# RWKV stage: the chunk's inverse folded into the state-side operand before the recurrence, so that a step leaves the product stream twice

## The chip, the cores and the metric

One core of one Trainium2 chip runs the whole program. The metric is the device time of one execution in microseconds (us), median of several runs.

## The reference, cut to what matters

One inference step of a hybrid backbone on 512 sample tokens and 128 prompt tokens (640 in all, 2048 wide): a large input product, two branches (RWKV-7 with 16 heads of 64, and an RG-LRU), gates, output products and norms. The change is in the RWKV branch, which runs forward and backward over the tokens of each head:

```python
def step(s, inp):
    r_t, w_t, k_t, v_t, kk_t, a_t = inp
    s_kk = jnp.einsum('bhvk,bhk->bhv', s, kk_t)
    s = s * w_t[:, :, None, :] - s_kk[..., None] * (kk_t * a_t)[:, :, None, :] + v_t[..., None] * k_t[:, :, None, :]
    return s, jnp.einsum('bhvk,bhk->bhv', s, r_t)
```

The kernel computes this by chunks of 64 tokens. In a chunk the vectors u (what each token takes from the state and from the tokens before it) solve a triangular system: u = Q (N S + M V), with S the state at the chunk's start, V the values, M a masked matrix of tokens against tokens, and Q the inverse of a unit triangular 64x64 matrix. With u known, the new state and the outputs y are plain products.

## The kernel before, in words

The program is one stream of large products on PE with all other work hung into it by hand. `piece` issues six matmuls for each 128 rows of a product's depth (L327: three of the split pairs high x high, high x low, low x high, each for two halves of 320 tokens), and then calls `tick`, which gives one turn to each of three queues of Python generators: `front` (mixing r, k, v), `side` (the recurrence `rwkv`) and `back` (`normed`, which prepares the next pair of heads, and `norm`, which finishes the last one). A generator that says `yield from idle(n)` lets n turns pass. So the numbers in W, INV, QI, X1 to X3 (before) or W, MV, MX, IW, INV, QI, X1, X2 (after) are turns between two pieces of side work, and they set the order of every engine's instructions. Each engine works its own list strictly in that order; SP issues nearly all transfers, in its own order too. A product of depth 2048 has 16 turns.

The RWKV stage goes through eight pairs of heads, i = 0 to 7. Pair i is worked while the products of host i run: for i = 1 to 5 these are seven (three gates m, r, k and v of the next pair, and ga), 112 turns; host 0 has nine, host 6 eight, host 7 seven (six gates and ga). `rwkv(i)` is put on `side` when host i begins.

What `rwkv(i)` does before the change, in this order:
- The decayed operands are written to `st4` (L835, L836), in pieces.
- `values`: ten transposes of v (L983) and copies into `sv`.
- `first` (L930) multiplies b against both decayed operands, 128 columns, six times; `bring` masks the two halves (L936, L937) into `at` and `rb`. `send` writes `at` to DRAM.
- The blocks are read back to `xn` and `xi`, 32x32 blocks on 104 partitions, which ScalarE turns (L1064, L1067). VectorE inverts them by 30 rounds of two instructions (L1072, L1074). Between the rounds `second` (L948, masked by L954) and `turned` (L964) are worked, for the k side.
- The inverses go out (L1081, L1085) and come back (L1093, L1099); two rounds of 32x32 products (L1108, L1122) make the whole Q in `qm`.
- Eight steps of the recurrence, forward and backward chunks at once (four chunks and heads wide in the first two steps, two wide after). A step leaves the product stream three times: `px` and part of `py` (L1141, L1145), then a copy `xt_` (L1148) and `pu` = Q x (L1153), then `pn` (L1162) and the rest of `py` (L1166). Copies by `put` (L1000, L1001) hand u and the state on.

On PE "an excursion" below is one such departure from the stream of L327 and the return to it. PSUM has four one-bank buffers `rw` for all of this. A line shown as x16 for fp32 operands is eight matmuls in the program: each is recorded as two.

Of the kernel before, what the change touches and what calls it, by code (L numbers as in the profile page):

```python
# [45 lines left out]
W = (2, 2, 2, 2, 2, 2, 2, 2, 2, 1, 3, 2)  # L46
INV = (0, 1, 1, 1, 1, 1, 1, 1, 2, 2, 2, 2, 2, 2, 2, 2)
QI = (1, 5, 7, 3, 1)
X1 = (1, 2, 1, 1, 2, 1, 1, 1)
X2 = (2, 2, 2, 2, 2, 1, 2, 2)  # L50
X3 = (3, 2, 2, 2, 3, 1, 2, 1)
NI = (1, 2, 1, 1)

# [10 lines left out]
C_ID, C_MSK, C_SEL, C_SCAN = 0, 128, 384, 386  # L64
# [6 lines left out]
def _consts():  # L71
    c = np.zeros((P, C_END), np.float32)
    p = np.arange(P)
    j = (p % CH)[:, None]
    t = np.arange(CH)[None, :]
    c[:, C_ID:C_ID + P] = np.eye(P)
    c[:, C_BLK:C_BLK + P] = (p[:, None] // CH == p[None, :] // CH)
    c[:, C_MSK:C_MSK + 256] = np.concatenate([j < t, j <= t, j > t, j >= t], 1)
    c[:, C_SEL:C_SEL + 2] = p[:, None] % 32 == np.arange(2)[None, :]
    c[:, C_SCAN:C_SCAN + CH] = t != 0  # L80
    return c
# [53 lines left out]
def step_kernel(ctx: ExitStack, tc: tile.TileContext, xt, w_in, w_a, w_b, w_o, ws, lw2, ada_w, ada_g, ada_b, cond, condr, gains,  # L135
# [569 lines left out]
    with tc.tile_pool(name="rwkv", bufs=1) as rp:  # L705
        def slot(name, dtype=F32):
            return rp.tile([P, SLOT], dtype, tag="rs", name=name, bufs=13)

        def mixed(q, i):
# [17 lines left out]
            def mix():  # L727
# [7 lines left out]
                s = slot("sh")  # L735
                sv = chunks(s)
                V.tensor_tensor(sv[:, 0:8], zr[:, :, 0:64], zr[:, :, 2:66], ALU.add)
                yield
                V.tensor_tensor(sv[:, 1:8], sv[:, 1:8], zr[:, 0:7, 1:65], ALU.add)
                yield  # L740
                V.tensor_tensor(sv[:, 0:7], sv[:, 0:7], zr[:, 1:8, 1:65], ALU.add)
                yield
                V.tensor_tensor(s[:, TS:T], zp[:, 0:128], zp[:, 2:130], ALU.add)
                V.scalar_tensor_tensor(o[:, :TS], s[:, :TS], dc(3 + q, i), o[:, :TS], ALU.mult, ALU.add)
                V.scalar_tensor_tensor(o[:, TS:T], s[:, TS:T], dc(6 + q, i), o[:, TS:T], ALU.mult, ALU.add)
# [11 lines left out]
        mask = [c[:, C_MSK + P * d:C_MSK + P * (d + 1)].rearrange("p (a t) -> p a t", a=2) for d in range(2)]  # L757
# [12 lines left out]
        class Scan:  # L770


            def __init__(self, i, k, r):
                self.i, self.k, self.r, self.nk = i, k, r, None
                self.th, self.pin, self.pex, self.kd, self.bk, self.st4 = ([None, None] for _ in range(6))
# [54 lines left out]
            def decayed(self, d, n0=0, n1=NC):  # L830

                n = slice(n0, n1)
                for e in range(2):
                    sl = hd(e)
                    V.tensor_tensor(self.st4[d][sl, n, e, 0], chunks(self.nk)[sl, n], self.pex[d][sl, n], ALU.mult)  # L835
                    V.tensor_tensor(self.st4[d][sl, n, e, 1], chunks(self.r)[sl, n], self.pin[d][sl, n], ALU.mult)  # L836
# [20 lines left out]
        def normed(i, k, r):  # L857
# [49 lines left out]
            z.bonus = kds  # L907
            ready[i] = z

        def rwkv(i, v):  # L910
# [6 lines left out]
            st4s = z.st4 = [rp.tile([P, NC, 2, 2, CH], F32, tag=f"st4{d}", name="st4") for d in range(2)]  # L917
            rbs = [rp.tile([P, NC, CH], F32, tag=f"rb{d}", name="rb") for d in range(2)]
            toks = [rp.tile([P, NC, 2, CH], F32, tag=f"tok{d}", name="tok") for d in range(2)]
            ats = [None, None]  # L920
            pcs = z.pcs

            def first(d, n0):

                nn = min(4, NC - n0)
                pa, m = ps1(), nn * P
                for n in range(n0, n0 + nn):
                    x = P * (n - n0)
                    for e in range(2):
                        PE.matmul(pa[hd(e), x:x + P], z.bk[d][hd(e), n, e],  # L930
                                  st4s[d][hd(e), n, e].rearrange("p a t -> p (a t)"), start=True, stop=True)

                def bring():
                    mb = mask[d].unsqueeze(1).to_broadcast([P, nn, 2, CH])
                    pav = pa[:, :m].rearrange("p (c a t) -> p c a t", a=2, t=CH)
                    V.tensor_tensor(chunks(ats[d])[:, n0:n0 + nn], pav[:, :, 0], mb[:, :, 0], ALU.mult)  # L936
                    V.tensor_tensor(rbs[d][:, n0:n0 + nn], pav[:, :, 1], mb[:, :, 1], ALU.mult)  # L937
# [3 lines left out]
            def second(d, n0):  # L941

                nn = min(4, NC - n0)
                pb, m = ps1(), nn * P
                for n in range(n0, n0 + nn):
                    x = P * (n - n0)
                    for e in range(2):
                        PE.matmul(pb[hd(1 - e), x:x + P], z.bk[d][hd(e), n, 1 - e],  # L948
                                  st4s[d][hd(e), n, e].rearrange("p a t -> p (a t)"), start=True, stop=True)

                def bring(e):
                    mb = mask[d].unsqueeze(1).to_broadcast([P, nn, 2, CH])
                    so = hd(1 - e)
                    V.tensor_tensor(st4s[d][so, n0:n0 + nn, e],  # L954
                                    pb[so, :m].rearrange("p (c a t) -> p c a t", a=2, t=CH), mb[so], ALU.mult)

                return lambda: bring(0), lambda: bring(1)
# [120 lines left out]
            for _ in work:  # L1078
                pass
# [363 lines left out]
```

## Time and profile before

| what | value |
|---|---|
| median of three runs | 2220.9 us (2217.12 to 2221.93) |
| the profiled execution: its time, its span | 2224.06 us, 2222.3 us |
| mean granted TensorE clock | 0.979 of 2.4 GHz |
| busy: PE, DVE, ACT, POOL | 2102.0, 1373.5, 976.0, 876.1 us |

The span runs from the first to the last instruction; 1.8 us lie around it. Busy time of PE counts modelled ends of pipelined matmuls, so a stretch in which PE is "busy" throughout can still hold lost time, and starts of successive instructions are the better measure.

### The profile page before, as it was taken

What the parts mean: (1) busy time and instruction counts of PE and PEld (TensorE: products, weight loads), DVE (VectorE), ACT (ScalarE), POOL (GpSimd) and SP (SyncE); (2) the same over time, 40 slices, a digit from 0 to 9 for tenths busy, and PEclk for the clock granted to TensorE, in tenths of its full rate; (3) what the DMA queues carried; (4) which work ended last, traced back from release to release, by engine and by line L of the source; (5) the groups of instructions that cost most, each with busy time, mean ns of one, the idle gap of its engine ahead of it and who ended that gap; (6) DMA issues with size and microseconds to landing.
All of it is one profiled execution on the core that took longest, in us unless ns stands there. A gap on an engine that the chain in (4) does not pass through costs nothing.

```text
span 2222.3 us, 47521 instructions
## 1 busy us (share of the span) xinstructions
PE 2102.0 (95%) x18236; PEld 1960.5 (88%) x18236; DVE 1373.5 (62%) x2665; ACT 976.0 (44%) x2264; POOL 876.1 (39%) x1164
## 2 busy tenths in 40 slices
PE   3999999999998998998998989989999899999997
PEld 2789999998888898898888888989988799999997
DVE  5655765696747756666676477665532699733354
ACT  4336776643433444444334434444333422234554
POOL 1244545553333333433333333334323455543343
PEclk8999999999999999999999999999999899999999
DMA  8953334332322222223123232232222766644474
GB/s 335 337 183 133 119 115 137 97 99 75 97 67 77 92 81 84 72 77 95 60 74 99 76 92 71 78 88 79 87 85 75 251 223 227 186 147 154 151 240 154
DMA packets 203507, 281.64 MB, mean 127 GB/s; under 512 B 69360, under 2 KB 91056, under 8 KB 202768
## 3 DMA queue, kind: packets, MB, share of 16 engines
q1 hardware_dynamic: 202832, 277.38, 39.2%
q8 instruction: 144, 2.36, 0.4%
q0 software_dynamic: 448, 1.23, 0.2%
q14 instruction: 83, 0.68, 0.1%
HBM read 237.70 MB, written 39.85 MB: 125 GB/s over the span
## 4 chain that ended last, share of the span: by engine, by line
PE 71%; DVE 19%; DMA 4%; issue 3%; ACT 2%; SPq 1%; POOL 1%; DVEq 0%; ACTq 0%; POOLq 0%
PE pj L327 52%; DVE tmp L1072 3%; DVE xi L1074 3%; PE rw L563 3%; DVE junk L1321 2%; PE rw L479 2%; PE rw L930 2%; DVE gws L1323 1%; DVE st L954 1%; PE ada L381 1%; PE pj L479 1%; PE rw L1153 1%; PE rw L1141 1%; PE rw L1166 1%; PE rw L948 1%
## 5 line engine op out<-in xcount | busy, mean ns | idle before, releaser
L310 POOL TENSOR_TENSOR wl<-wr,wh 128x256 fp32r<-128x256 f32 x922 | 790.9, 866 | 1255.8 <-ACT wh L309 1199.9
L327 PE MATMUL pj<-xh,wh 128*128 128x320 f32 (+2 forms) x2976 | 761.8, 323 | 2.3 <-ACT wh L309 2.3
L327 PE MATMUL pj<-xh,wl 128*128 128x320 f32 (+2 forms) x2976 | 724.5, 311 | 2.0 <-DVE wl L310 1.5
L327 PE MATMUL pj<-xl,wh 128*128 128x320 f32 (+2 forms) x2976 | 724.8, 311 | 0.0
L309 ACT ACTIVATE wh<-wr 128x256 fp32r<-128x256 f32 x1048 | 421.4, 413 | 517.4 <-PE pj L327 396.5
L327 PEld LDWEIGHTS pj<-xh,wh 128*128 128x128 f32 x2976 | 502.9, 190 | 34.5 <-issue 14.3
L327 PEld LDWEIGHTS pj<-xh,wl 128*128 128x128 f32 x2976 | 512.8, 189 | 3.7 <-DVE wl L310 2.5
L327 PEld LDWEIGHTS pj<-xl,wh 128*128 128x128 f32 x2976 | 513.3, 189 | 0.1
L1072 DVE TENSOR_TENSOR tmp<-xn,xi 104x30 f32<-104x30 f32 (+14 forms) x240 | 100.0, 417 | 82.6 <-ACT xn L1067 76.1
L1001 DVE COPY sv<-rw 64x128 f32<-64x128 f32 x80 | 23.6, 295 | 198.0 <-ACT sv L1000 196.8
L310 DVE TENSOR_TENSOR wl<-wr,wh 128x256 fp32r<-128x256 f32 x126 | 57.6, 459 | 127.1 <-ACT wh L309 126.9
L1074 DVE TENSOR_TENSOR xi<-xi,tmp 104x30 f32<-104x30 f32 (+14 forms) x240 | 99.9, 416 | 8.2
L1321 DVE SCALAR_TENSOR_TENSOR junk<-gws,cb 128x512 f32<-128x512 f32 x64 | 67.5, 1055 | 10.1 <-ACT cb L1313 10.1
L327 PE MATMUL pj<-yah,wh 128*128 128x320 f32 x256 | 59.6, 315 | 8.1 <-ACT g L1234 8.1
L954 DVE TENSOR_TENSOR st<-rw,c 64x512 f32<-64x512 f32 (+1 forms) x96 | 57.6, 600 | 12.4 <-PE rw L948 10.2
L1323 DVE SCALAR_TENSOR_TENSOR gws<-gws,cb 128x512 f32<-128x512 f32 x64 | 61.5, 961 | 1.9
L327 PE MATMUL pj<-yah,wl 128*128 128x320 f32 x256 | 59.4, 314 | 0.5 <-POOL wl L310 0.5
L327 PE MATMUL pj<-yal,wh 128*128 128x320 f32 x256 | 59.2, 313 | 0.0
L327 PE MATMUL pj<-ybh,wh 128*128 128x320 f32 x256 | 58.5, 310 | 0.4 <-DVE thx L1357 0.4
L327 PE MATMUL pj<-ybh,wl 128*128 128x320 f32 x256 | 58.5, 309 | 0.3 <-POOL wl L310 0.3
L327 PE MATMUL pj<-ybl,wh 128*128 128x320 f32 x256 | 58.3, 309 | 0.0
L1000 ACT ACTIVATE sv<-rw 64x128 f32<-64x128 f32 x80 | 21.7, 271 | 74.7 <-PE rw L1153 68.9
(767 smaller groups left out, 3077.6 us busy)
## 6 DMA issues: line engine op xcount, KB each, us to landing
wr<-w_in SPq DMA_DIRECT2D x312, 256.0 KB
adaw<-ada_w SPq DMA_DIRECT2D x64, 512.0 KB
wr<-w_o SPq DMA_DIRECT2D x128, 256.0 KB
gws<-ada_g SPq DMA_DIRECT2D x64, 256.0 KB
thl<-th SPq DMA_DIRECT2D x32, 320.0 KB
th<-thl SPq DMA_DIRECT2D x32, 320.0 KB
thm<-g SPq DMA_DIRECT2D x64, 160.0 KB
thx<-thm SPq DMA_DIRECT2D x32, 320.0 KB
```

The costliest lines, as they stand in the source:

```text
L309: S.activation(h, r, AF.Copy)
L310: lows[pos[1] % len(lows)].tensor_tensor(lo, r, h.bitcast(F32), ALU.subtract)
L327: PE.matmul(p[:, :t1 - t0], w, x[:, t0:t1], start=(k == 0 and a == 0), stop=(k == nk - 1 and a == 2))
L479: PE.matmul(p[:, :HT], u[:, w], x[:, t], start=new, stop=end)
L563: PE.matmul(p, a, b, start=(n == 0), stop=(n == 2))
L930: PE.matmul(pa[hd(e), x:x + P], z.bk[d][hd(e), n, e], st4s[d][hd(e), n, e].rearrange("p a t -> p (a t)"), start=True, stop=True)
L954: V.tensor_tensor(st4s[d][so, n0:n0 + nn, e], pb[so, :m].rearrange("p (c a t) -> p c a t", a=2, t=CH), mb[so], ALU.mult)
L1001: V.tensor_copy(sv[hd(1), a, 1], src[hd(1), b])
L1072: V.tensor_tensor(t, xn[:NV, j, j + 1:].unsqueeze(2).to_broadcast([NV, m, j]), xi[:NV, j, :j].unsqueeze(1).to_broadcast([NV, m, j]), ALU.mult)
L1074: V.tensor_tensor(xi[:NV, j + 1:, :j], xi[:NV, j + 1:, :j], t, ALU.add)
L1321: V.scalar_tensor_tensor(junk, w, 1.0, cbs[h][:, 0], ALU.mult, ALU.mult, accum_out=gs[:, h, n, 0:1])
L1323: V.scalar_tensor_tensor(w, w, 1.0, cbs[h][:, 1], ALU.mult, ALU.mult, accum_out=gs[:, h, n, 1:2])
```

## The change

The inverse Q is multiplied into the operand [N^T; M^T] of each chunk ahead of the recurrence (`fold`), for all chunks. A step then gets u in one product of depth 128 from state and values together (`pu`), and the copy `xt_` is gone; all the rest of the step is one more excursion. The state's part of y is a product of its own now with a decayed r (`z.rp`). `first` makes 64 columns; the other products of tokens against tokens are made by `across` and `outward`, for which b and k of both heads stand in one stationary operand where that can be; a second mask `smk` lets the unmasked state side through. `decayed` is done once for whole rows in `normed`. The mixing of r, k, v is written with multiply-adds into the result and without the buffer `sh`. All turn counts are new; `turned` is moved behind the inverse.

Turns of `rwkv(i)` counted from these tuples, from its start: before, the inverse begins at turn 24, its write (L1085) is at 48, the reads at 53, L1108 at 60, the first step at 64, the end at 105. After: `first` at 0 and 2, `across` at 5, 7, 9 and 12, the inverse at 11, `outward` at 17, 22, 28 and 45, the write at 45, the reads at 47, L1108 at 51, `fold` and `turned` from 55, the first step at 63, the end at 100.

```diff
+W, SD, LD = (2, 0), 0, (1, 3)
+MV, MX = (1, 2, 2, 2), 2
+IW = (2, 5, 7, 9)
+INV = (0, 1, 1, 2, 2, 3, 2, 3, 3, 2, 3, 3, 2, 2, 2, 2)
+QI = (1, 2, 4, 2, 2, 1, 1, 1)
+X1 = (2, 2, 2, 2, 1, 2, 1, 2)
+X2 = (3, 3, 3, 3, 3, 3, 3, 2)
...
+                ov, m4, m2 = chunks(o), dc(3 + q, i), dc(6 + q, i)
+                for x, y in ((ov[:, 0:8], zr[:, :, 0:64]), (ov[:, 0:8], zr[:, :, 2:66]), (ov[:, 1:8], zr[:, 0:7, 1:65]),
+                             (ov[:, 0:7], zr[:, 1:8, 1:65])):
+                    V.scalar_tensor_tensor(x, y, m4, x, ALU.mult, ALU.add)
+                    yield
...
+            def decayed(self, d):
+
+                t = self.r if d else slot("rp")
+                V.tensor_tensor(chunks(t), chunks(self.r), self.pin[d], ALU.mult)
+                V.tensor_tensor(self.pex[d], chunks(self.nk), self.pex[d], ALU.mult)
+                self.rp[d], self.nkp[d] = chunks(t), self.pex[d]
...
+            def both(n0):
+                for n in range(n0, n0 + 5):
+                    for e in range(2):
+                        yield n, e, slice(CH * (n - n0), CH * (n - n0 + 1))
...
             def first(d, n0):
+                pa = ps1()
+                for n, e, x in both(n0):
+                    PE.matmul(pa[hd(e), x], z.bk[d][hd(e), n, e], z.nkp[d][hd(e), n], start=True, stop=True)
                 def bring():
+                    V.tensor_tensor(ats[d][:, n0:n0 + 5], five(pa), wide(mask[d][:, 0]), ALU.mult)
...
+            def across(d, n0):
+                pq = [ps1(), ps1()]
+                for n, e, x in both(n0):
+                    PE.matmul(pq[e][hd(e), x], z.nkp[d][hd(e), n], ident[hd(e), hd(e)], start=True, stop=True)
+                for n, e, x in both(n0):
+                    PE.matmul(pq[1 - e][hd(e), x], z.nkp[d][hd(e), n], z.bk[d][hd(e), n, 1 - e], start=True, stop=True)
+                for h in range(2):
+                    V.tensor_tensor(sws[d][:, n0:n0 + 5, h], five(pq[h]), wide(smk[d][:, h]), ALU.mult)
+
+            def outward(d, n0):
+                po = [ps1(), ps1()]
+                for n, e, x in both(n0):
+                    PE.matmul(po[e][:, x], z.bk[d][hd(e), n].rearrange("p a t -> p (a t)"), z.rp[d][hd(e), n],
+                              start=True, stop=True)
+                for e in range(2):
+                    V.tensor_tensor(ros[d][:, n0:n0 + 5, e], five(po[e]), wide(mask[d][:, 1]), ALU.mult)
...
+            def fold(d, n0):
+                pq = [ps1(), ps1()]
+                for n, e, x in both(n0):
+                    PE.matmul(pq[e][:, x], sws[d][hd(e), n].rearrange("p a t -> p (a t)"), qm[d][hd(e), n],
+                              start=True, stop=True)
+                S.activation(sws[d][:, n0:n0 + 5, 0], five(pq[0]), AF.Copy)
+                V.tensor_copy(sws[d][:, n0:n0 + 5, 1], five(pq[1]))
...
+            def moved():
+                values(0, 4)
+                values(4, 8)
+                yield
+                values(8, NC)
+                pb = heads([z.bonus])
...
+                for f in (across, outward):
+                    for d in range(2):
+                        for n0 in (0, 5):
+                            f(d, n0)
                             yield
...
+            for d in range(2):
+                bring = first(d, 0), first(d, 5)
+                for f in bring:
+                    f()
+                later(SD, lambda d=d: send(d))
+                yield from idle(W[d])
+
+            for n, (x, d) in enumerate(((xn[0:NB], 0), (xi[64:NV], 1))):
+                later(LD[n], lambda x=x, d=d: nc.sync.dma_start(x, sa[d][0].rearrange("g n r c -> (g n) r c")))
             work = moved()
+            for n in MV:
+                next(work)
+                yield from idle(n)
+            S.activation(xi[0:NB], xn[0:NB].rearrange("p j t -> p t j"), AF.Copy)
             next(work)
+            yield from idle(MX)
             S.activation(xn[64:NV], xi[64:NV].rearrange("p t j -> p j t"), AF.Copy)
...
                 if j % 2 == 0:
-                    next(work, None)
+                    if j // 2 in IW:
+                        next(work)
                     yield from idle(INV[j // 2])
...
-            yield from idle(QI[1])
+            for _ in work:
+                yield from idle(QI[1])
...
             yield from idle(QI[4])
+            for n in range(4):
+                fold(n % 2, n // 2 * 5)
+                yield from idle(QI[5])
+                turned(n % 2, n // 2 * 5)
+                yield from idle(QI[6] if n < 3 else QI[7])
...
             for s in range(8):
+                xe = [(x, e, slice(x * CH, (x + 1) * CH)) for x in range(np_) for e in range(2)]
+                pu = ps1()
+                for x, e, o in xe:
+                    PE.matmul(pu[hd(e), o], sws[x % 2][:, ch[x], e], sv[:, at(s, x), e], start=True, stop=True)
+                put(s, np_, pu[:, :np_ * CH].rearrange("p (a n) -> p a n", n=CH))
                 yield from idle(X1[s])
                 if s < 7:
                     pn = ps1()
+                    for x, e, o in xe:
+                        PE.matmul(pn[hd(e), o], toks[x % 2][:, ch[x], e], sv[:, at(s, x), e], start=True, stop=True)
+                py = ps1()
+                for x, e, o in xe:
+                    PE.matmul(py[hd(e), o], sv[:, at(s, x), e], ros[x % 2][:, ch[x], e], start=(x == 0), stop=False,
+                              skip_group_check=True)
+                for x, e, o in xe:
+                    PE.matmul(py[hd(e), o], sc_[hd(e), x], z.rp[x % 2][hd(e), ch[x]], start=False, stop=True,
+                              skip_group_check=True)
...
-                yield from idle(X3[s])
+                yield from idle(X2[s])
```

## Rows read from the trace of the kernel before

**Rows 1.** The page: busy time and share of each engine; the chain by engine.
```profile
PE 2102.0 (95%) x18236; PEld 1960.5 (88%) x18236; DVE 1373.5 (62%) x2665; ACT 976.0 (44%) x2264; POOL 876.1 (39%) x1164
...
PE 71%; DVE 19%; DMA 4%; issue 3%; ACT 2%; SPq 1%; POOL 1%; DVEq 0%; ACTq 0%; POOLq 0%
```

**Rows 2.** Windows over pair 3: length, then PE, PEld, DVE, ACT, POOL busy, clock.
```profile
940.60:976.10 35.50, 35.50 (x300) 31.97 (x300) 19.32 (x39) 17.92 (x37) 10.56 (x14) 1.00 0.30 81
976.10:1012.90 36.80, 36.28 (x285) 33.78 (x283) 34.62 (x79) 11.50 (x33) 12.42 (x23) 1.00 0.18 56
1012.90:1020.90 8.00, 1.66 (x77) 1.45 (x79) 3.90 (x10) 2.07 (x5) 2.77 (x4) 0.70 0.57 141
1020.90:1026.30 5.40, 5.40 (x44) 5.00 (x36) 0.00 (x0) 2.75 (x6) 2.24 (x2) 0.50 0.52 115
```

**Rows 3.** Waits of PE in the stage: total us, times, longest.
```profile
PE rw L1108 <- DMA xi<-scr: 41.0, 11, 6.7
PE rw L1141 <- ACT sv L1000: 7.6, 6, 1.3
...
PE rw L854 <- DVE st L954: 3.0, 1, 3.0
```

**Rows 4.** Timeline of pair 3 around the inverse: start, duration, instruction.
```profile
973.96 2.12 ACT L1067 ACTIVATE xn<-xi 40x1024 f32<-40x1024 f32 x1
...
1011.84 0.30 SPq L1085 DMA_DIRECT2D scr<-xi  x1
...
1019.09 2.13 PE L1108 MATMUL rw<-xi,at 32*32 32x32 f32 x80 [6.71 <-DMA xi<-scr]
...
1019.95 1.14 PEld L1108 LDWEIGHTS rw<-xi,at 32*32 32x32 f32 x74 [0.23 <-DMA xi<-scr]
```

**Rows 5.** Timeline of PE at four excursions, with the products beside them.
```profile
877.79 0.46 PE L327 MATMUL pj<-xl,wh 128*128 128x320 f32 x2
878.08 0.46 PE L327 MATMUL pj<-xh,wl 128*128 128x320 f32 x2
878.47 0.68 PE L1153 MATMUL rw<-xt__10729,qm 64*64 64x64 f32 x16
879.08 0.56 PE L327 MATMUL pj<-xh,wh 128*128 128x320 f32 x2
879.48 0.46 PE L327 MATMUL pj<-xl,wh 128*128 128x320 f32 x2
...
884.72 0.46 PE L327 MATMUL pj<-xh,wl 128*128 128x320 f32 x2
...
886.19 0.56 PE L327 MATMUL pj<-xh,wh 128*128 128x320 f32 x2
...
890.32 0.46 PE L327 MATMUL pj<-xh,wl 128*128 128x320 f32 x2
...
891.94 0.56 PE L327 MATMUL pj<-xh,wh 128*128 128x320 f32 x2
...
947.29 0.46 PE L327 MATMUL pj<-xh,wl 128*128 128x320 f32 x2
...
948.70 0.56 PE L327 MATMUL pj<-xh,wh 128*128 128x320 f32 x2
```

**Rows 6.** Groups of DVE instructions in pair 3: busy us, mean ns.
```profile
L1074 DVE TENSOR_TENSOR xi<-xi,tmp 104x30 f32<-104x30 f32 (+14 forms) x30 | 13.9, 462 | 1.0
L1072 DVE TENSOR_TENSOR tmp<-xn,xi 104x30 f32<-104x30 f32 (+14 forms) x30 | 10.8, 361 | 11.6 <-ACT xn L1067 10.8
L954 DVE TENSOR_TENSOR st<-rw,c 64x512 f32<-64x512 f32 (+1 forms) x12 | 7.2, 600 | 2.0 <-PE rw L948 1.7
...
L835 DVE TENSOR_TENSOR st<-nk,pw 64x256 f32<-64x256 f32 (+1 forms) x8 | 5.2, 645 | 0.1
...
L936 DVE TENSOR_TENSOR at<-rw,c 128x256 f32<-128x256 f32 (+1 forms) x6 | 2.2, 374 | 2.8 <-PE rw L930 2.7
...
L1215 DVE SCALAR_TENSOR_TENSOR gs<-rw,gs 128x320 f32<-128x320 f32 x2 | 0.9, 487 | 0.0
```

More of the change, by code (lines that the diff above doesn't have):

```diff
@@ L907, in normed @@
             z.bonus = kds
+            for d in range(2):
+                yield
+                z.decayed(d)
+            z.th = z.kd = z.pin = z.pex = z.k = z.r = z.nk = None
             ready[i] = z
@@ L921, in rwkv, with five @@
             pcs = z.pcs
-            def first(d, n0):
[L925 to L931, printed above, removed]
+            def five(p):
+                return p[:, :HT].rearrange("p (c t) -> p c t", t=CH)
@@ L1005, in rwkv @@
             G.memset(sc_[:, 2:4], 0.0)
-            values(0)
-            yield from idle(W[0])
-            values(1)
-            bring = first(0, 0)
-            z.decayed(0, 4)
-            yield from idle(W[1])
-            ats[0] = slot("at")
-            bring()
-            bring = first(0, 4)
-            z.decayed(1, 0, 4)
-            yield from idle(W[2])
-            bring()
-            bring = first(0, 8)
-            z.decayed(1, 4)
-            yield from idle(W[3])
-            bring()
@@ L1023, in rwkv @@
-            z.pin = z.pex = None
-            later(2, lambda: send(0))
-            bring = first(1, 0)
-            yield from idle(W[4])
-            ats[1] = slot("at")
-            bring()
-            bring = first(1, 4)
-            pb = heads([z.bonus])
-            yield from idle(W[5])
-            bring()
-            bring = first(1, 8)
-            yield from idle(W[6])
-            bring()
-            for s in range(2):
-                h = slice(s * HT, (s + 1) * HT)
-                V.tensor_tensor(v[:, h], v[:, h], pb[s][:, :HT], ALU.mult)
@@ L1040, in rwkv @@
-            later(2, lambda: send(1))
-            later(2, lambda: nc.sync.dma_start(xn[0:NB], sa[0][0].rearrange("g n r c -> (g n) r c")))
-            def moved():
-                for d in range(2):
-                    for n0 in (0, 4, 8):
-                        for bring in second(d, n0):
-                            yield
-                            bring()
-                        if n0 < 8:
-                            yield
-                            turned(d, n0 // 4 * 5)
-                        yield
+            def moved():
+                values(0, 4)
+                values(4, 8)
+                yield
+                values(8, NC)
+                pb = heads([z.bonus])
+                for s in range(2):
+                    h = slice(s * HT, (s + 1) * HT)
+                    V.tensor_tensor(v[:, h], v[:, h], pb[s][:, :HT], ALU.mult)
+                z.bonus = None
+                yield
+                for f in (across, outward):
+                    for d in range(2):
+                        for n0 in (0, 5):
+                            f(d, n0)
+                            yield
@@ L1147, in rwkv @@
-                xt_ = rp.tile([P, 4 * CH], F32, tag="xt", name="xt_", bufs=1).rearrange("p (a n) -> p a n", n=CH)
-                S.activation(xt_[:, :np_], px[:, :np_ * CH].rearrange("p (a n) -> p a n", n=CH), AF.Copy)
-                yield from idle(X1[s])
-                pu = ps1()
-                for x in range(np_):
-                    for e in range(2):
-                        PE.matmul(pu[hd(e), x * CH:(x + 1) * CH], qm[x % 2][hd(e), ch[x]], xt_[hd(e), x], start=True,
-                                  stop=True)
```

133 lines of the change are left out of this document (30 added, 103 removed).

## The prediction, made before the result was known

> **What bounds the kernel now.** I read the page first: PE is busy 95% of the span and carries 71% of the chain, DVE 19% [rows 1]. So the time is PE's own work plus the places where PE stands still. The waits of PE inside the RWKV stage then name one large place: the first product behind the inverse, L1108, waits 41.0 us in all for the inverse to come back from DRAM; L1141, which opens a step, waits 7.6 us for the state's copy; a wait for a PSUM buffer that VectorE had yet to read occurs once, 3.0 us [rows 3]. Windows over one pair (pair 3, begun at 940.60) show why L1108 waits: in the 36.8 us from the first round of the inverse to its last copy VectorE is busy 34.62, so VectorE sets the end of the inverse; PE then has work for 1.66 of 8.00 us, and after that 5.40 us pass at half of the 2.4 GHz clock [rows 2]. The same picture stands in pairs 1 to 6, and milder in pair 7.
>
> The rest of the stage is PE's own issue. In the timeline a pair of L327 matmuls starts every 0.29 us (877.79, 878.08) [rows 5], so one turn of three pairs is 0.88 us. What side work costs is how much later the stream resumes. Around L1153 the pairs start at 878.08, 879.08 and 879.48: 1.40 us where two strides would be 0.59, so this excursion of 16 records costs 0.81. Sixteen records of 64 columns stream in 0.42 (64 columns at 2.4 GHz are 0.027 each); leaving and coming back cost 0.39. The excursion of L1141 and L1145 (884.72 to 886.19, and the same late second pair) costs 1.28 for 32 records, that of L1162 and L1166 (890.32 to 891.94) 1.43, 0.20 of it because the 64-row products follow 128-row ones in it, and 16 records of 128 columns in L930 (947.29 to 948.70) 1.22, again 0.39 and 0.83 of streaming [rows 5].
>
> **The change, part by part, for one pair of heads.**
>
> *The recurrence.* Before, a step costs 1.28 + 0.81 + 1.43 = 3.52 when four wide (two steps) and, with half the records, 0.81 + 0.60 + 1.01 = 2.42 when two wide (six). After, `pu` alone is 0.81 or 0.60, and the second excursion holds 48 records with the same inner change of rows: 0.39 + 1.25 + 0.20 = 1.84, or 1.22. A step is 2.65 or 1.82. Saved: 2 x 0.87 + 6 x 0.60 = 5.3 us.
>
> *Ahead of it.* Gone: `first` and `second` with 128 columns, four excursions of 16 records and two of 8 each: 2 x (4 x 1.22 + 2 x 0.80) = 13.0. New: `first` with 40 records per direction in one excursion, 0.39 + 1.05 = 1.44, twice; `across` the same size, four times; `outward` and `fold` 20 records each, 0.91, four times each. Together 2.9 + 5.8 + 3.6 + 3.6 = 15.9. PE pays 2.9 more. `turned`, L1108 and L1122 are moved and cost the same. `values` is cut in two pieces and the bonus product rides with the second, so no piece is added that was not one before.
>
> Net on PE: 2.9 - 5.3 = -2.4 us a pair, about -19 over eight.
>
> The trace gives no sign that products in different quarters of the array overlap: 16 records of 64 rows by 64 take the full 0.42 us [rows 5]. The Trainium skill, TensorEngine Tiling (Array Packing), section Key Properties, says that tiles work independently and load and multiply in parallel. By that the 64-row records would cost half, on both sides of the account; removed and added nearly cancel, and the sum would be about 4 us lower than mine.
>
> *VectorE and the inverse.* `decayed` falls from 16 operations of at most 0.645 us (L835) to four whole rows, and leaves the front of `rwkv`. `bring` of `first` is four reads of PSUM at about 0.49 us (L1215, 128x320) for twelve at 0.37 (L936). `second` had twelve at 0.600 (L954, 7.2 us); `across` and `outward` have sixteen at 0.49, but six of `across` come ahead of the inverse and the last two of `outward` behind it, so eight (3.9 us) stand between its rounds [rows 6]. The mixing keeps its count of operations of each size: nothing. `fold` adds four reads each to ScalarE and VectorE; ScalarE loses the eight copies `xt_`.
>
> *When the inverse ends.* Before: it starts 35.5 us after the pair [rows 2]. After: turn 11 is reached at 11 x 0.88 + 2.9 (`first`) + 2.0 (`values` and bonus, my estimate from their 14 records beside the excursions above) + 4.3 (three `across`) = 18.9; ScalarE's second copy, 2.12 us (L1067) [rows 4], ends at 21. The blocks sent to DRAM and back need not be later: `first` is done at turn 2, and nine turns lie before that copy. Then 13.9 + 10.8 of rounds [rows 6], 3.9 of masks, and 4.1 of mixing and last copy (what is left of the 34.62 busy us when rounds and the ten L954 of that stretch, 5.8, are taken off [rows 2, 6]): the inverse is ready at 53.7. PE reaches the write's place, turn 45, at 39.6 + 2.9 + 2.0 + 5.8 + 2.7 = 53.0. So VectorE is no longer late by more than about a microsecond.
>
> *What the wait becomes.* The way out and back remains: from the first write (1011.84) to the bulk of L1108's weight loads (1019.95) 8.1 us [rows 4]. Cover between write and L1108 shrinks from 12 turns to 6 turns and one `outward`: 5.3 + 0.9 = 6.2. PE therefore waits 53.7 + 8.1 - 53.0 - 6.2 = 2.6 us instead of some 6. SP's list holds nothing new between write and reads but the weight loads of two turns. The loss in clock should shrink with the wait; I put 1.4 us on it where the window shows 5.4 us at half rate, so 2.7 lost [rows 2], in pair 3; as a mean over the pairs I take 2.2, an estimate a little below it. Seven pairs: before 41.0 + 7 x 2.2 = 56, after 7 x 4.0 = 28; gain 28. Bounds: nothing (VectorE late again) and 56 (way fully covered).
>
> *Steps.* A state now has three turns to pass through add, scaling and copies, where it mostly had two: the 7.6 us of L1141 [rows 3] should go; I count 7.
>
> *New waits.* Each pair now has twelve pieces of work that take PSUM buffers two at a time (`across`, `outward`, `fold`), each behind two evictions. By the turns between them they should find buffers. No row shows them; bounds 0 and 3.0 us a piece (the one PSUM wait of [rows 3]). I take the near end, half a microsecond a pair, 4 us in all, because the one wait occurred where VectorE was 35 of 37 us busy.
>
> *Small.* The constants grow by 128x256 words, 131 KB in the first load. Two halves of a weight piece are no reason for a term; if uncovered, it shifts the start by less than a microsecond. Pair 7 ends five turns earlier, which shortens the drain; not counted.
>
> Sum against the profiled execution: 2224.06 - 19 - 28 - 7 + 4 = 2174. That execution lies 3.2 us above the median of 2220.9, so 2171 on that footing; with the drain and the lighter VectorE both pulling down uncounted, I say **2168 us**, its own range 2152 to 2184.
>
> **The rivals.**
>
> *The way is covered.* If VectorE finishes before turn 45 (every figure above holds contention with POOL, and six `across` masks are ahead of time), and the writes land a little quicker, the wait and its clock loss vanish: 2168 - 28 = 2140.
>
> *VectorE stays late.* The slack between 53.7 and 53.0 is thin; the mixing of r falls among the rounds, and PE is now faster. Late by four more microseconds, L1108 waits as before: 2168 + 28 = 2196.
>
> *Evictions become the bound: slower.* `across`, `outward` and `fold` make twelve pieces a pair that each need two of four PSUM buffers and two reads by VectorE or ScalarE, and VectorE's list is in order behind the rounds. Without new waits the sum is 54 us faster, so the point is 54 / 96 = 0.56 us a piece. At 1.0 us a piece: 2168 - 4 + 96 = 2260. Against it: only one such wait, of 3.0 us, in the whole stage before [rows 3]. The Trainium skill, TensorEngine Tiling (Array Packing), section PSUM Bottleneck, speaks for this rival: tiled products do not speed up the emptying of PSUM, which may become the bottleneck, and both ScalarE and VectorE should share it. `across` and `outward` leave it to VectorE alone.
>
> *No change.* `rwkv` falls from 105 to 100 turns, but a host has 112 either way; a stage bound by hosts would not move. It moves only because PE fills the hosts' time with excursions and waits [rows 2, 5], so I give this little: 2221.
>
> **How the numbers follow.** Forecast 0.49; way covered 0.18; VectorE stays late 0.18; evictions 0.12; no change 0.03. Measurement tells 0.2% (4.4 us) from no change. Faster: 0.49 + 0.18 + 0.18 = 0.85; within 0.2%: 0.04 (no change, and the edge of the late case); slower: 0.11. The range takes in both faster rivals with their spread and leaves out the evictions' case and the tails: 2130 to 2212. Forecast's own range stands above.
>
> **What would show it.** Excursions: between L327 pairs, two a step, some 0.8 and 1.8 us when four wide. Inverse: L1072 starts about 21 us after the pair's first instruction, and the write L1085's counterpart leaves as PE passes turn 45; the wait in front of L1108's counterpart is 2 to 3 us, seven times, with a half-rate stretch shorter than 5 us. Each pair of heads from 1 to 6 lasts some 6 to 7 us less than before. Wrong would be: waits of PE for VectorE or ScalarE ahead of `across` or `fold`; L1108 still waiting 6 us; or `pu` waiting for `put` in each step.

## The result and the profile after

The change made the kernel slower: 2234.4 us (median of four runs, 2232.0 to 2235.7) against 2221.0, a ratio of 1.0062, 95% interval 1.0045 to 1.008. Forecast were 2168 us and a range of 2130 to 2212. The profiled execution took 2233.4 us, with a span of 2231.6 where before it was 2222.3.

The page's row of busy times answers to [rows 1]:

```profile
PE 2124.3 (95%) x19516; PEld 2003.4 (90%) x19516; DVE 1351.8 (61%) x2569; ACT 978.5 (44%) x2232; POOL 873.5 (39%) x1164
```

TensorE has 1280 more matmul records and is busy 22 us longer, although the waits were meant to fall. VectorE is busy 22 us less.

The waits of PE in the stage (total us, times, longest) answer to [rows 3]:

```profile
PE rw L1140 <- DVE sv L1014: 13.9, 7, 3.5
PE rw L1095 <- DMA xi<-scr: 10.0, 16, 2.6
PE rw L855 <- POOL yl L843: 9.6, 6, 1.8
PE rw L945 <- DVE pw L836: 7.4, 1, 7.4
PE rw L1095 <- DVE k L743: 2.7, 2, 1.7
```

The big wait did go: L1108's 41.0 us are L1095's 10.0 and 2.7. L1141's 7.6 are gone too: L1133, which opens a step now, waits 0.6 us in all. In their place stand two that were not there: L1140 (it opens the second excursion of a step) waits for VectorE's copy of u, and L855, the normalisation's head sums, waits for POOL. L945's wait stands once, at the start of pair 0; before, L930's there was of 3.1 us.

Windows of pair 3 (begun at 955.10 now), cut where [rows 2] were cut: to the first round of the inverse, to its last copy, to the stream's return behind the products with it, and a stretch behind. Columns as there:

```profile
955.10:972.97 17.87, 17.87 (x263) 16.41 (x260) 10.59 (x20) 10.40 (x21) 5.08 (x7) 1.00 0.43 107
972.97:1011.71 38.74, 38.74 (x336) 37.45 (x335) 34.53 (x77) 10.02 (x27) 14.97 (x26) 1.00 0.23 73
1011.71:1019.20 7.49, 5.95 (x113) 5.54 (x111) 5.26 (x11) 2.27 (x7) 1.76 (x2) 1.00 0.57 139
1019.20:1024.40 5.20, 5.08 (x126) 4.53 (x112) 0.23 (x1) 3.95 (x10) 0.73 (x1) 1.00 0.50 95
```

While the inverse is away PE has work for 5.95 of 7.49 us (1.66 of 8.00 before), and the granted clock stays at 1.00 there and behind it (0.70 and 0.50 before). VectorE is still busy for 34.53 of the inverse's 38.74 us. The inverse begins 17.9 us after the pair (forecast 21), and its first write leaves at 1010.16, 55.1 us after it (forecast 53.7). This half of the forecast came in.

The timeline of PE at one `outward`, with the stream beside it, answers to [rows 5]:

```profile
980.25 0.46 PE L332 MATMUL pj<-xh,wl 128*128 128x320 f32 x2
980.63 1.33 PE L966 MATMUL rw<-rp,bk 64*128 64x64 f32 x20
981.90 0.56 PE L332 MATMUL pj<-xh,wh 128*128 128x320 f32 x2
982.30 0.45 PE L332 MATMUL pj<-xl,wh 128*128 128x320 f32 x2
```

From 980.25 to 982.30 are 2.05 us where two strides would be 0.59: the excursion costs 1.46 us, where the forecast had 0.91. An `across` of twice as many records costs hardly more (963.63 to 965.74; 1.51 by the starts before rounding, as the median of all 32):

```profile
963.63 0.46 PE L332 MATMUL pj<-xh,wl 128*128 128x320 f32 x2
964.02 0.80 PE L956 MATMUL rw<-c,pw 64*64 64x64 f32 x20
964.65 0.75 PE L958 MATMUL rw<-bk,pw 64*64 64x64 f32 x20
965.33 0.57 PE L332 MATMUL pj<-xh,wh 128*128 128x320 f32 x2
965.74 0.46 PE L332 MATMUL pj<-xl,wh 128*128 128x320 f32 x2
```

Over the whole stage I took the starts of PE's weight loads and summed, for each excursion, the time by which the stream comes back later than its stride of 0.147 us a product record. Waits and lost clock are in these sums. In the last two columns five of the normalisation's excursions fall together with `values` and stand, with some 5 us, in the row ahead of the recurrence. In us, with three kernels of the experiments beside the two:

```
                                 before   after  both_narrow  wide_lists  later_lists
steps of the recurrence           178.9   148.2      149.0       140.1       140.0
first product with the inverse     59.0    26.7       32.7        26.9        41.0
second                              8.4     9.9       12.0        10.3         9.5
ahead of the recurrence, fold     128.5   193.3      160.2       197.8       164.0
turned                             20.9    20.8       20.8        20.8        20.8
norm, where by itself              13.0    22.5       22.5         6.5         6.5
gaps inside the stream             18.3    15.7       17.4        10.3        13.2
sum                               427.0   437.0      414.3       412.7       395.0
span of the execution            2222.3  2231.6     2208.9      2208.7      2191.9
```

The sums tell the spans: 10 more after, and the span is 9.3 longer. The steps give 31 and the inverse's wait 32; the work ahead of the recurrence takes 65 where 23 were forecast (2.9 a pair), and the normalisation 10.

### The profile page after: what moved, and what is told of

Same layout as the page of the kernel before. It is cut to its first block, busy times and chain, and to the rows that moved or that the text cites. A ratio compares the mean times of both kernels' runs of the same rounds, so it can differ in the third digit from the quotient of the medians.

```text
span 2231.6 us, 49821 instructions
## 1 busy us (share of the span) xinstructions
PE 2124.3 (95%) x19516; PEld 2003.4 (90%) x19516; DVE 1351.8 (61%) x2569; ACT 978.5 (44%) x2232; POOL 873.5 (39%) x1164
## 5 line engine op out<-in xcount | busy, mean ns | idle before, releaser
L1061 DVE TENSOR_TENSOR xi<-xi,tmp 104x30 f32<-104x30 f32 (+14 forms) x240 | 107.5, 448 | 8.2
L985 DVE COPY sw<-rw 128x320 f32<-128x320 f32 x32 | 15.7, 491 | 140.5 <-PE rw L982 140.5
L960 DVE TENSOR_TENSOR sw<-rw,c 128x320 f32<-128x320 f32 x64 | 28.4, 485 | 47.1 <-PE rw L958 47.1
```

Of the source, the lines that this page charges most:

```text
L960: V.tensor_tensor(sws[d][:, n0:n0 + 5, h], five(pq[h]), wide(smk[d][:, h]), ALU.mult)
L985: V.tensor_copy(sws[d][:, n0:n0 + 5, 1], five(pq[1]))
L1061: V.tensor_tensor(xi[:NV, j + 1:, :j], xi[:NV, j + 1:, :j], t, ALU.add)
```

## The experiments

Ratios are to the kernel before, which was timed on the same chip beside each run.

**Order of the products.** Theory then: a product of 64 columns runs beside its neighbour when the two go to different halves of the array's columns, and the rows from which I priced had this overlap in them. The edit takes the alternation out:

```diff
-                for n in range(n0, n0 + 5):
-                    for e in range(2):
+                for e in range(2):
+                    for n in range(n0, n0 + 5):
...
-                xe = [(x, e, ...) for x in range(np_) for e in range(2)]
+                xe = [(x, e, ...) for e in range(2) for x in range(np_)]
```

> The changed kernel with the products of first, across and of every step ordered by head (all of one column half of PE, then all of the other), where they alternated; fold and outward keep their order in kind. Theory (two fp32 products run at once when they go to different column halves of the array, and a 128-column stationary fills both): each of these products falls from sharing to taking its full time, 0.053 us more for each of 20 in first (twice), 20 pairs in across (four times) and 156 in the steps of a pair of heads, some 14.6 us a pair and 117 in all, so about 2350 us, with records of L1133 two by two 0.11 us apart instead of 0.058. Rival (the load of 128 weight columns is what makes fold and outward dear, not the halves): order is of no matter, 2234 us.

Measured: 2318.5 us, one run, 1.042 times the kernel before, where the changed kernel is at 1.006: slower by some 80 us, where the theory had 117 and the rival nothing. The same `outward` in the timeline:

```profile
1012.92 0.46 PE L332 MATMUL pj<-xh,wl 128*128 128x320 f32 x2
1013.30 2.05 PE L966 MATMUL rw<-rp,bk 64*128 64x64 f32 x20
1015.28 0.56 PE L332 MATMUL pj<-xh,wh 128*128 128x320 f32 x2
1015.68 0.45 PE L332 MATMUL pj<-xl,wh 128*128 128x320 f32 x2
```

It now costs 2.17 us (1012.92 to 1015.68, less 0.59), an `across` 2.13 instead of 1.51. The starts of single records say why: in the changed kernel two records start 0.007 us apart and the next two 0.058 later (0.112 in `outward`); in this order each starts 0.058 (0.112) behind the last, but for the few where the two runs meet. So neighbours do run side by side. But `outward` should not have moved by a theory of column halves alone: its stationary of 128 columns fills both, and only its rows alternate. Rows overlap too. (`outward` and `fold` go through `both` as well, so the edit reorders them: their 64 excursions, 0.71 dearer each, are 45 us that the theory did not have.) The products that the theory did price lost less than it said. In an `across` of this order the second run of products (L958) begins while three records of the first (L956) have still to start, although the program has all of the first ahead of it:

```profile
995.02 0.27 PE L958 MATMUL rw<-bk,pw 64*64 64x64 f32 x1
995.07 0.22 PE L956 MATMUL rw<-c,pw 64*64 64x64 f32 x1
...
995.19 0.22 PE L956 MATMUL rw<-c,pw 64*64 64x64 f32 x1
```

The second excursion of a step two wide, where only four records of one head follow each other in each product, costs 1.25 in place of 1.19.

**A narrow outward.** The stationary of `outward` holds b and k of one head (not of both, as the section on the change has it). It is cut in two:

```diff
-                for n, e, x in both(n0):
-                    PE.matmul(po[e][:, x], z.bk[d][hd(e), n].rearrange("p a t -> p (a t)"), z.rp[d][hd(e), n], ...)
+                for n, e, x in both(n0):
+                    for w in range(2):
+                        PE.matmul(po[e][hd(w), x], z.bk[d][hd(e), n, w], z.rp[d][hd(e), n], ...)
```

> The changed kernel with outward's 64x128 stationary (b and k of a head together) split into two of 64x64, one for each column half: twice as many products. Theory of the halves: two narrow ones at once cost what the wide one does, so 0 (2234 us, within 4). Rival, which is the price in the prediction (a record of 64 columns costs 0.026 us whatever its stationary): 20 records more for each of 32 excursions, 17 us slower, 2251.

Measured: 2225.7 us, ratio 1.0011 [0.9998, 1.0024], by the ratios some 11 us less than the changed kernel, which neither side had expected. Twice as many records take less time:

```profile
979.00 0.46 PE L332 MATMUL pj<-xh,wl 128*128 128x320 f32 x2
979.39 0.81 PE L967 MATMUL rw<-rp,bk 64*64 64x64 f32 x40
980.13 0.56 PE L332 MATMUL pj<-xh,wh 128*128 128x320 f32 x2
980.53 0.45 PE L332 MATMUL pj<-xl,wh 128*128 128x320 f32 x2
```

The excursion costs 0.94 us (979.00 to 980.53, less 0.59). Four records start within 0.02 us, and the next four 0.058 later: all four quarters of the array (a half of the rows by a half of the columns) work at once. So the theory of two column halves fell, and this one took its place: **every quarter runs its own product.** A narrow record holds one quarter for 0.058 us. A wide one holds two for 0.112.

**Turns.** Two runs ask whether the waits can be moved by turns alone. In the changed kernel, three more turns ahead of the products with the inverse, two ahead of step four's second excursion, two ahead of the normalisation (pairs 0 to 6); in the kernel before, six turns ahead of L1108, which uses 111 of the host's 112 (the first line below with 6 in place of 3, and that line alone):

```diff
-            yield from idle(QI[2])
+            yield from idle(QI[2] + (3 if i < NT - 1 else 0))
...
-                yield from idle(X1[s])
+                yield from idle(X1[s] + (2 if s == 4 and i < NT - 1 else 0))
...
-            yield from idle(HP[2])
+            yield from idle(HP[2] + (2 if i < NT - 1 else 0))
```

> The changed kernel with other turn counts alone, for pairs 0 to 6: three turns more ahead of the first product behind the inverse, two more between the two excursions of step 4, two more ahead of norm's first product. Theory (PE's waits there are real time, and the host has turns to spare): some 14 us less in front of the inverse, 12 in step 4, 10 in front of norm's products, together 30 to 37, about 2200. Rival (the waits hide behind something else, or move to the next product): less than 10, 2225 or more.

> The kernel before with one count alone changed: six turns more ahead of L1108 for pairs 0 to 6 (111 of 112 turns used). Theory (its 7 us of waiting and the clock after it are a matter of turns, not of the algebra): 5 to 7 us less in each of six pairs, 30 to 42 in all, 2179 to 2191. Rival (VectorE sets the pace of the pair; what is saved there is waited for later): under 10, 2211 or more.

Measured: 2224.0 us, ratio 1.0000 [0.9991, 1.0009], and 2242.3 us, ratio 1.0084 [1.007, 1.0098]. The waits of PE, first in the changed kernel with more turns, then in the kernel before with more turns:

```profile
PE rw L1140 <- DVE sv L1014: 23.5, 12, 3.3
...
PE rw L1095 <- DMA xi<-scr: 1.6, 4, 0.6
```

```profile
PE pj L327 <- ACT wh L309: 32.2, 7, 6.0
...
PE rw L1108 <- DMA xi<-scr: 3.8, 2, 3.6
```

The first is 14 us under the changed kernel by the ratios, nearer to the rival (under 10) than to the theory (30 to 37). L1095's waits are down from 12.7 to 1.6 and L855's 11.3 are gone, but L1140's have grown from 13.9 to 23.5, and two more of 2.4 and 2.5 us stand in the steps: more than half of the gain is taken by the steps. In the second, L1108's 41.0 are 3.8, but the stream itself now waits 32.2 us for its weights' upper halves from ScalarE. ScalarE's list shows why, in pair 3 of this run and of the kernel before:

```profile
1023.27 0.74 ACT L864 ACTIVATE q<-nk 128x640 f32<-128x640 f32 x1 [13.53 <-DVE nk L862]
```

```profile
1016.97 0.74 ACT L864 ACTIVATE q<-nk 128x640 f32<-128x640 f32 x1 [11.89 <-DVE nk L862]
```

L864 waits for VectorE, whose L862 stands behind the inverse and the mixing of k, and the next upper halves (L309) stand behind L864. So the rival won, by way of ScalarE: six turns more do not help the kernel before, because VectorE holds the stream at the next place. Fewer turns, or VectorE's list spread in the kernel before, were not tried.

**Fold, and both.** The fold is cut as `outward` was, alone and together with it:

```diff
-                    PE.matmul(pq[e][:, x], sws[d][hd(e), n].rearrange("p a t -> p (a t)"), qm[d][hd(e), n], ...)
+                    for w in range(2):
+                        PE.matmul(pq[e][hd(w), x], sws[d][hd(e), n, w], qm[d][hd(e), n], ...)
```

> The changed kernel with only the fold's 64x128 stationary cut into two of 64x64, both column halves one behind the other for the same rows; the outward product stays wide. Outward alone came down from 1.46 to 0.94 us an excursion when it was cut like this. Theory (a product whose stationary has 128 columns lasts twice as long as one whose stationary has 64, and narrow products in all four quarters run at once, so the same work takes half the time): the fold falls from 1.46 to about 0.94, 32 times, 16.6 us of the tensor engine's time, and since nothing waits ahead of the fold about 10 to 15 of it is seen: a ratio of 0.999 to 1.001 to the kernel before. Rival (outward was a special case, for example because its moving side is fresh from the vector engine; the fold's cost is its count of records): the fold grows by 20 records, 1.46 to about 1.98, and the time rises by 17, a ratio of 1.013.

> The changed kernel with the outward product and the fold both on 64x64 stationaries, so without the shared stationary of both heads' b and k; everything else of the change stays. Theory: both at 0.94 an excursion, 33 us less on the tensor engine than the changed kernel's wide forms; with the third that came back as a wait behind the inverse in the run of outward alone, 20 to 28 us are seen: 2206 to 2214 where the changed kernel is 2234, a ratio of 0.990 to 0.995 to the kernel before: the sign that was forecast. Rival (the wide stationary was not what cost the gain, the added waits behind the normalisation and in step four were): the saved time returns as waits, 2220 to 2230, a ratio of 1.000 to 1.004.

Measured: the fold alone 2220.8 us, ratio 0.9977 [0.9968, 0.9986], a little more than its theory had; its excursion fell from 1.46 to 0.94. Both: 2211.9 us, ratio 0.9946 [0.9933, 0.9958], within the theory's range. With the wide stationaries alone undone, the change makes the kernel faster, as forecast in sign. The table shows 33 us less ahead of the recurrence, and 6 of them back in front of the inverse's products.

**Two quarters.** Narrow products in an order that keeps only two quarters side by side (`outward`: alternating rows; fold: alternating columns), shown against the version with both narrow:

```diff
-                for n, e, x in both(n0):
-                    for w in range(2):
+                for w in range(2):
+                    for n, e, x in both(n0):
                         PE.matmul(po[e][hd(w), x], ...)
...
-                for n, e, x in both(n0):
+                for e in range(2):
+                    for n in range(n0, n0 + 5):
                     for w in range(2):
                         PE.matmul(pq[e][hd(w), ...], ...)
```

> Both products on 64x64 stationaries as in the run before this one, but in an order in which only two of the four quarters stand next to each other: outward all of one column half and then all of the other, alternating between the two halves of the rows; the fold all of one half of the rows and then all of the other, alternating between the column halves. Theory (what a narrow product gains, it gains by the neighbours that run in other quarters; records 58 ns apart, two starting together instead of four): both excursions at 0.39 + 20 x 0.058 = about 1.5 us, as dear as the wide form, a time of 2230 to 2240. Rival (the narrow form is cheaper by itself, whatever stands beside it): both stay at 0.94 and the time is that of the run before this one.

Measured: 2233.0 us, one run, 1.003 times the kernel before: far from the 0.995 of the good order and nearly back at the 1.006 of the wide stationaries. One `outward` of this order:

```profile
982.72 0.46 PE L332 MATMUL pj<-xh,wl 128*128 128x320 f32 x2
983.11 1.21 PE L967 MATMUL rw<-rp,bk 64*64 64x64 f32 x40
984.25 0.56 PE L332 MATMUL pj<-xh,wh 128*128 128x320 f32 x2
984.65 0.45 PE L332 MATMUL pj<-xl,wh 128*128 128x320 f32 x2
```

The same 40 records cost 1.34 us (0.94 with four quarters). Two start together every 0.058 us, except where the first run ends and the second begins: there four do for two groups, so it is 1.34 and not the 1.5 expected. The narrow form is not cheaper by itself; the neighbours in other quarters are what it gains by.

**VectorE's list.** What is left of the loss is in the two new waits. The timeline of the changed kernel in step four of pair 2, VectorE first, then PE:

```profile
916.87 1.08 DVE L830 TENSOR_TENSOR bk<-kd,th 64x384 f32<-64x384 f32 x1
917.99 1.97 DVE L743 SCALAR_TENSOR_TENSOR v<-z,dv,v 128x512 f32<-128x512 f32 x2
919.99 0.29 DVE L1014 COPY sv<-rw 64x128 f32<-64x128 f32 x1
```

```profile
916.52 0.45 PE L1133 MATMUL rw<-sv,sw 128*64 128x64 f32 x8
...
920.34 0.39 PE L1140 MATMUL rw<-sv,tok 128*64 128x64 f32 x5 [2.04 <-DVE sv L1014]
```

`pu` is done at 916.97, but VectorE's half of the copy stands in its list behind an `over` of the next pair and two passes of v's mixing, and starts at 919.99. At the end of the pair:

```profile
939.84 0.82 DVE L835 TENSOR_TENSOR rp<-r,pw 128x640 f32<-128x640 f32 x1
940.69 1.25 DVE L836 TENSOR_TENSOR pw<-nk,pw 128x640 f32<-128x640 f32 x1
941.97 0.29 DVE L1163 TENSOR_TENSOR ysum<-ysum,rw 128x128 f32<-128x128 f32 x1
```

The last sum of y is behind `decayed`, which the change put there as whole rows; L855 waits for what follows from that sum. Neither seems to be needed so early. Two edits to the version with both products narrow:

```diff
             def mix():
...
+                yield from idle(2 if q == 2 and i else 0)
                 ov, m4, m2 = chunks(o), dc(3 + q, i), dc(6 + q, i)
...
             for d in range(2):
-                yield
+                yield from idle(5 if i else 1)
                 z.decayed(d)
```

The second run starts the products with the inverse two turns later as well.

> The version with both products on 64x64 stationaries, and VectorE's list spread at the two places where the tensor engine still waits for it in the recurrence: v's mixing starts two turns later (in the version before this it stands in step four ahead of the copy of the values, five pairs of eight, 2 us of waiting and 1.5 of a lower clock each), and the two products that make the decayed keys and rates of the next pair start five turns later (they stand ahead of the last sum of y, behind which the normalisation waits, 1.6 to 1.9 us in six pairs). Theory (the list's order alone makes these waits, the engine has free time right behind them): step four's 3.55 to 5.8 stalls fall to 1.9, the normalisation's 2.5 to about 0.6, some 10 to 20 us less on the tensor engine, 5 to 15 seen: a ratio of 0.988 to 0.993 to the kernel before. Rival (VectorE is full in the recurrence, a moved wait comes up in another step, as it did when the whole was shifted): no change against 0.9946 within 0.002.

> As the run before this one, and the products with the inverse two turns later (pairs zero to six), where the tensor engine waits 15 us for the inverse's rows to come back in the version with both products narrow. Theory (with VectorE's list spread the steps no longer take up what this frees): the wait ahead of the products falls from 33 to about 20 and 4 to 8 us more are seen, a ratio of 0.985 to 0.990. Rival (the later start is given back by the steps, as when the changed kernel was shifted): the same time as the run before this one, within 2 us.

Measured: 2193.4 us, ratio 0.9864 [0.9852, 0.9877], a larger gain than expected; and 2206.6 us, ratio 0.9919 [0.9904, 0.9935]. The waits of PE, with later lists:

```profile
PE rw L1096 <- DMA xi<-scr: 16.0, 15, 5.0
PE rw L1096 <- DVE nk L864: 9.2, 3, 3.1
...
PE rw L1141 <- DVE sv L1015: 5.9, 6, 2.5
```

and with two turns more:

```profile
PE rw L1096 <- DMA xi<-scr: 14.0, 17, 6.7
PE rw L1141 <- DVE sv L1015: 12.9, 7, 2.2
```

The order of the lists made most of the two waits: L855 (L856 here) is down from 11.3 to 0.4, L1141 (L1140 before the edit) from 13.9 to 5.9. (The lower clock that the expectation puts beside the wait in step four is not there: the granted clock is 1.00 from 917.6 to 925 in pair 2, and the rest of its 3.55 us is nearly all the excursion itself, 1.19.) More turns are given back, as the rival said and beyond: by the starts of the loads 12 us less stand in front of the inverse's products and some 18 more in the steps. So 2193.4 us is the best version tried, 1.4% under the kernel before.

**The lists alone**, with the wide stationaries kept, to part the causes:

> The changed kernel with its wide stationaries as they are, and only VectorE's list spread as in the version with the later lists (v's mixing two turns, the decayed products five turns later). It parts the two causes. Theory (the wide forms cost the kernel some 22 us and the order of VectorE's list some 18, each by itself): 2212 to 2220, a ratio of 0.995 to 0.999 to the kernel before. Rival (the later lists pay only where the tensor engine is no longer the bound ahead of the recurrence): within 5 us of the changed kernel, a ratio of 1.004 or more; or, if the lists are the whole cause and the wide forms cost nothing once they are spread: that of the version with later lists, 0.986.

Measured: 2210.8 us, ratio 0.9935 [0.9922, 0.9949], a little below the theory's range and at neither rival's value. The four kernels side by side, as ratios to the kernel before:

```
                     lists as changed   later lists
wide stationaries         1.0062          0.9935
narrow stationaries       0.9946          0.9864
```

Each edit by itself turns the change from slower to faster: the quarters are worth 26 us, or 16 with the lists spread; the lists 28, or 18. Some 10 us are in both: the less PE is held up, the earlier it is at the inverse, and waits there (the table's 26.9 us for wide and 41.0 for narrow stationaries, both with later lists).

## Why the prediction was wrong

Measured by the book-keeping, the forecast missed by 60 us: 50 less were forecast (-19, -28, -7, +4), 10 more came.

- *The wait for the inverse: right, with some luck.* Forecast a gain of 28 with its clock, book-kept 32; in pair 3 the rows show waits of about 1.5 us where I had 2.6, and no stretch at half of the clock. But VectorE's end was 1.4 us later than forecast there, and PE itself came 1.5 us late to the place of the write (the `outward` right behind it begins at 1009.64, 54.5 us after the pair, where I had 53.0), because three `outward` ahead of it cost 0.55 more each. With both products narrow the row is 32.7, with later lists 41.0: a gain of 18 is left of the 32.
- *The steps: right in size, without the new stalls.* I had 1.84 us for the second excursion when four wide and 1.22 when two wide; most of them measured 1.88 and 1.19. The 7 us for L1141's wait came in.
- *`outward` and `fold` at 0.91: the step that failed first.* They cost 1.46 each, 64 times: 35 us. I took 0.026 us a record, 64 columns at 2.4 GHz, for all shapes of 64 columns, because the excursions came out so when divided by their records. But the rows of [rows 5] were of products whose stationaries have 64 columns and alternate between the halves: a record came every 0.058 us, two at a time. A record of the wide form came every 0.112, also two at a time. Seen so, one wide product equals two narrow ones, and what it takes away is the chance to fill four quarters. That is what the wide stationaries of `outward` and `fold` cost.
- *"The trace gives no sign that products in different quarters of the array overlap": wrong.* The sign stood in the same rows, in starts 0.007 and 0.058 apart, and I read their mean. The Trainium skill, TensorEngine Tiling (Array Packing), section Key Properties, says that tiles can load and multiply in parallel; the runs agree, with four starts within 0.02 us. I set it aside, and where I worked it out I halved both sides of the account (done again with the prediction's own terms, the two sides cancel to less than 1 us, not to 4), without seeing that the products priced already ran two at a time and that a stationary 128 columns wide takes two quarters.
- *`across` and `first` at 1.44:* 1.51 measured, 48 times, 3 us.
- *New waits at 4 us: wrong in place and size.* The twelve pieces with two PSUM buffers, on which I put them, show almost none (the one row of PE for the fold is 0.4 us), so the rival of the evictions, to which I had given most of the chance of a slower kernel, did not happen either: the sign was slower for another reason. The waits came where I put none. I moved `decayed` and the mixing at the cost of their busy time, and did not ask what stands behind them in VectorE's list: a step's copy of u (about 16 us, five times 2.3 in step four and once some 4 in pair 0) and the last sum of y (10 us). That VectorE had less to do altogether, 22 us, did not matter.
- *Pair 0:* its first product waits for `decayed` in the old place of `first`: 7.4 where 3.1 were, 4 us.
- *Rivals:* "VectorE stays late" named the right engine and the wrong place.

These terms make the 60: 35 + 16 + 10 + 4 + 3 is 68, less the 4 that I had put on waits in PSUM and the 4 by which the wait for the inverse gave more. The mended version does not reach the forecast either: its sum is 32 under the kernel before, where 50 were forecast. Ahead of the recurrence it has 35 more, where 23 were forecast, and the wait for the inverse gives 18 where 28 were forecast.

What stays open is why a record of `outward` takes twice as long with 128 columns in its stationary as with 64 (0.112 and 0.058, also when nothing runs beside it). The width alone is not it. `turned` has the same 64x128 stationary and 64 columns, but as a transposition, and there two records start together every 0.060 us. The weight loads' rows of pair 3 (form of the stationary, count, then busy us and mean ns of one) go the same way:

```profile
L956 PEld LDWEIGHTS rw<-c,pw 64*64 64x64 f32 x80 | 2.6, 134 | 0.8 <-issue 0.8
L966 PEld LDWEIGHTS rw<-rp,bk 64*128 64x128 f32 x40 | 2.4, 187 | 0.4 <-issue 0.4
L974 PEld LDWEIGHTS rw<-c,bk 64*128 64x128 f32 x40 | 1.6, 138 | 0.8 <-ACT wh L314 0.4 <-issue 0.4
```

`outward`'s load (L966) lasts 0.053 us longer than that of a narrow stationary (L956), as its stride is 0.054 longer, and `turned`'s (L974) does not. So the load may set the pace; no run shows it. Whether the kernel before would gain from a spread list of VectorE by itself is open too. The start of pair 0 was not mended.

## What to carry to other kernels

Before you price a small matmul by records, look at the starts of single records: is each as long as the stride, or do two or four begin together? A form that halves the instruction count by a wider stationary may only take away a neighbour's place. And when work is moved off the front of a stage, look where it lands in the other engine's list and which copy now stands behind it; an engine that is busy for less time in all can still hold up the one that sets the end.

## What the runs showed of the hardware

- fp32 products of 64 columns, 64 rows deep: on one quarter of the array a record every 0.058 us; on two alternating quarters (of rows or of columns) two records in 0.058; on all four, four. The excursion of the same 20 products cost 1.34 us with two and 0.94 with four. With all products of one quarter in a row and then all of the next, the overlap was left only where the two runs met: there the later one started ahead of the last three records of the earlier.
- A wide stationary (64x128): a record every 0.112 us, two at once when the rows alternate (excursion 1.46), one when they don't (2.17). As a transposition (`turned`) the same shape went two at once every 0.060 us (0.65 for ten records).
- The order of the products in the program was worth some 80 us (1.042 against 1.006 of the kernel before, the first from one run) with the same instructions.
